# A Mamba-2 layer's gated norm: the last group's scale applied behind the output product, its squares added on GpSimd, and the mixer norm's two scales computed ahead of its tiles

## The chip, the cores and the metric

One core of a Trainium2 chip. Its engines are TensorE (PE, matrix products into PSUM), VectorE (DVE), ScalarE (ACT), GpSimd (POOL) and the engine that issues transfers (SP). Each runs its own row of instructions in a fixed order and waits on semaphores for the others. The metric is the device time of one execution in microseconds (us), the median of several runs.

## The reference

A two-layer decoder trunk on 576 tokens (512 of a prompt, 8 x 8 of samples), width 1024, float32. Layer 0 has a convolution and attention mixer, layer 1 a Mamba-2 mixer; behind each stands a convolutional feed-forward block. Cut to what the change touches:

```python
def rmsnorm(x, g):
    xf = x.astype(jnp.float32)
    xf = xf * lax.rsqrt(jnp.mean(xf * xf, axis=-1, keepdims=True) + EPS)
    return xf.astype(x.dtype) * g
...
def odd_mixer(h, conv_hist, ssm_hist, w_in, conv_w, conv_b, dt_bias, a_log, d_skip, gn_g, w_out):
...
    y, new_ssm = ssd_scan(xs, dt, a, bm, cm, ssm_hist)
    y = (y + d_skip[:, None] * xs).reshape(b, t, D_INNER) * jax.nn.silu(z)
    gs = D_INNER // SSM_GROUPS
    y = rmsnorm(y.reshape(b, t, SSM_GROUPS, gs), gn_g.reshape(SSM_GROUPS, gs)).reshape(b, t, D_INNER)
    return y @ w_out, new_conv, new_ssm
...
            dp, c1, s1 = odd_mixer(rmsnorm(xp, norm_mix_o[i]),
                                   jnp.zeros((bp, SSM_CONV_WIDTH - 1, SSM_CONV_DIM), dty),
                                   jnp.zeros((bp, SSM_HEADS, SSM_HEAD_DIM, SSM_STATE), dty), *ow)
...
        xp = xp + dp
...
        fp, f1 = conv_ffn(rmsnorm(xp, norm_ffn[layer]), jnp.zeros((bp, FFN_CONV_WIDTH - 1, D_FF), dty), *fw)
...
        xp = xp + fp
```

The gated norm is taken over each of 4 groups of 512 channels: its scale is one number per token and group. So is a norm's scale in general one number per token (`rs` below, 1/sqrt of the mean square); the gain (`g`, `gn`) is one per channel.

## The kernel before

**Layout.** Channels lie on the 128 partitions, tokens along the free dimension. The stream x is eight tiles `x0` to `x7` of 128 x 576, in SBUF throughout (`x_77` to `x_84` in the rows below). Work runs in two halves of 288 tokens (`HALF`).

**Products.** Each float32 operand is split into a rounded high part and the low rest: weights in `weights` (`wr` as loaded, `wh` by ACT at L163, `wl` by DVE at L164), activations by `split` (high by ACT at L193, low by DVE at L194). A product is three matmuls per 128 x 128 block (`mm3`, L173 high by high, L174 low of the activation, L175 low of the weight), each over 288 tokens into a PSUM tile called `mm`.

**A norm.** Squares are made by ACT (L225 for the first tile, L228 for others) and added up by DVE (L229, in `sq_add`). `rstd` then sums over partitions on PE (L202, with a column of ones), takes root and reciprocal in small pieces (ACT L209, DVE L210, ACT L211, DVE L212 to L214), spreads the result over the partitions on PE (L218) and copies it out (ACT L220): this is `rs`, or `grs` in the gate. In an *early* norm (that of the first mixer, and those of the feed-forward blocks, `norm_f1` among them) `norm_tile` splits x times the gain into `hh` and `hl` at once (ACT L248, DVE L249), and the scale is applied behind the product. In the mixer's norm `norm_o`, not early, `norm_half` waits for the scale, makes scaled tiles `hf` (DVE L261) and splits them (`hh` L193, `hl` L194). Before, it does so for half 0 as soon as that half's scale is there, then for half 1. `hf` itself goes into a plain float32 product for the time steps (`quarters`, L182).

**The mixer.** `mix1` goes over 4 groups. For each it runs the scan (`ssd`) on four tiles `xs`, beside it the matmuls of projections, then `gate`: y = `xs` times silu of z (DVE L1266), squares and `rstd`, y times gain times scale (DVE L1270), split into `yh` and `yl`. The output product of a group runs beside the next group's scan; that of the last group has nothing beside it but the second half of group 2's (four of its eight tiles).

**The last projection.** `out_proj` with `norm=True` takes the last group's y, four blocks deep: 12 matmuls for each of 16 half tiles. `add_x` adds the product out of PSUM to x (DVE L288), and `norm_tile` at once works on the new x for `norm_f1`: split and square. Tiles 0 to 3 go half by half, tiles 4 to 7 first in half 0, then in half 1, so that the first half's scale is ready early. Then `norm_half`, and the first gate products of the feed-forward block.

**What sets the order.** The instructions are written in one order, and a scheduler moves them within each engine's row; the order written is their priority. SBUF tiles of 576 tokens come from numbered slots by `S()` and go back by `free()`, the one idle longest first, so a new tile may wait for the last reader of the old one. PSUM tiles `mm` rotate through four banks in the last projection. The norms' small matmuls L202 and L218 stand in PE's row between the matmuls of products, which wait behind them if they wait.

Of the kernel before, what the change touches and what calls it, by code (L numbers as in the profile page):

```python
# [8 lines left out]
F32 = mybir.dt.float32  # L9
F32R = mybir.dt.float32r  # L10
AF = mybir.ActivationFunctionType
# [39 lines left out]
class Builder:  # L51
# [170 lines left out]
    def sq_add(self, acc, src, first, sl):  # L222
        nc = self.nc
        if first:
            nc.scalar.activation(acc[:, sl], src, AF.Square)  # L225
        else:
            t = self.S("sq")
            nc.scalar.activation(t[:, sl], src, AF.Square)  # L228
            nc.vector.tensor_tensor(acc[:, sl], acc[:, sl], t[:, sl], op=ADD)  # L229
            self.free(t)  # L230
# [10 lines left out]
    def norm_tile(self, m, sl):  # L241

        nc = self.nc
        x = self.x[m][:, sl]
        if self.early:
            g = self.pv(self.gname, m)
            h, l = self.h[m]
            nc.scalar.activation(h[:, sl], x, AF.Copy, scale=g)  # L248
            nc.vector.scalar_tensor_tensor(l[:, sl], x, g, h[:, sl].bitcast(F32), op0=MUL, op1=SUB)  # L249
        self.sq_add(self.ssq, x, m == 0, sl)  # L250

    def norm_half(self, half):
# [3 lines left out]
        if not self.early:  # L256
            for k in range(8):
                if half == 0:
                    self.hf.append(self.S("hf"))
                t = self.hf[k]  # L260
                nc.vector.scalar_tensor_tensor(t[:, sl], self.x[k][:, sl], self.pv(self.gname, k), self.rs[:, sl],  # L261
                                               op0=MUL, op1=MUL)
                self.split(t[:, sl], self.h[k], sl)
        if half == 1:
            self.free(self.ssq)

# [18 lines left out]
    def add_x(self, m, half, p):  # L285
        nc = self.nc
        sl = HALF[half]
        nc.vector.tensor_tensor(self.x[m][:, sl], self.x[m][:, sl], p[:, :HB], op=ADD)  # L288

    def out_proj(self, srcs, xs, kper, norm=False, last_y=False):  # L290
# [6 lines left out]
        for m, hf in order:  # L297
# [5 lines left out]
            self.add_x(m, hf, p)  # L303
# [550 lines left out]
    def mix1(self):  # L854
# [400 lines left out]
        def gate(g, yv):  # L1255
# [7 lines left out]
            for half in (0, 1):  # L1263
                sl = HALF[half]
                for t in range(4):
                    nc.vector.tensor_tensor(yv[t][:, sl], yv[t][:, sl], zs[t][:, sl], op=MUL)  # L1266
                    self.sq_add(ssq, yv[t][:, sl], t == 0, sl)
                self.rstd(rs, ssq, self.o512[:, 0:32], sl)
                for t in range(4):
                    nc.vector.scalar_tensor_tensor(yv[t][:, sl], yv[t][:, sl], self.pv("gn", 4 * g + t), rs[:, sl], op0=MUL, op1=MUL)  # L1270
                    self.split(yv[t][:, sl], ys[t], sl)
            self.free(ssq, rs, yv, zs)
# [56 lines left out]
        self.out_proj([d["w_out_o"][3, c] for c in range(4)], ys, 4, True)  # L1329
        self.free(ys)  # L1330
# [176 lines left out]
```

## Time and profile before

| what | value |
|---|---|
| runs | 1550.84, 1553.37, 1554.91 us; median 1553.37 |
| the profiled execution | 1553.1 us |
| its span, first to last instruction | 1551.3 us |
| mean granted clock of TensorE | 0.997 |
| norm ahead of the mixer | about 632 to 659 us of the span |
| the four scans and gates | 659 to 1101 us |
| last projection, with norm_f1's tiles | about 1101 to 1127 us |
| second feed-forward block | from 1127 us on |

The profile is of one execution, so sums are made against 1553.1. "Busy" is the share of time in which an engine has an instruction under way. In a row of the timeline stand the start, the length, the engine, the line, the operation with out and in, the shape, how many instructions in a row are folded together, and in brackets how long the engine had been idle before and whose result ended that. Matmuls overlap by about half, so the length of one (0.29 us) isn't what it costs.

Over the whole span PE's waits are short and few; the largest kinds are

```profile
PE yp L1148 <- DVE acb L1118: 7.2, 5, 2.4
PE mm L173 <- ACT wh L163: 5.5, 2, 5.4
PE pst L1200 <- ACT ysb L1191: 1.9, 2, 1.3
PE mm L175 <- DVE wl L164: 1.8, 2, 1.3
PE pr L218 <- DVE dg L214: 1.6, 3, 1.2
PE mm L173 <- DVE x L288: 1.4, 2, 1.1
```

(who waited, for whom, us in total, times, the longest). The first are in the scan, the second is the start of the program.

### The profile page before, as it was taken

The numbers are of one execution on the slowest core, as the hardware profiler recorded it, in microseconds if no ns is written. First come the engines' busy times: TensorE is split into PE (matmuls) and PEld (weight loads), VectorE is DVE, ScalarE is ACT, GpSimd is POOL, SyncE is SP. The second block draws the span as 40 slices with busy tenths as digits, with TensorE's granted clock in tenths as the row PEclk, the third lists the DMA queues.
The fourth block names the chain that finished last, engine by engine and source line by source line (L and its number), as shares of the span: only waits on it lengthen the run. The fifth ranks groups of instructions, "written<-read, shape, count | busy, mean of one in ns | idle before, by whom it ended". The sixth has DMA issues, their size and how long they took to land.

```text
span 1551.3 us, 28549 instructions
## 1 busy us (share of the span) xinstructions
PE 1520.5 (98%) x11635; PEld 1449.8 (93%) x11635; DVE 1018.5 (66%) x1805; ACT 649.3 (42%) x1232; POOL 154.7 (10%) x365
## 2 busy tenths in 40 slices
PE   8999999999999999999999999999999999999999
PEld 7977799999999999898988988998999999999999
DVE  7969887553555464678896786777976644663552
ACT  6356553221222222486855654646632222321220
POOL 0036001000000000011211112102010000000000
PEclk9999999999999999999999999999999999999999
DMA  8515223222222222136245245245222222223222
GB/s 239 136 42 131 85 70 98 86 86 85 83 77 78 92 82 85 55 104 202 71 148 180 83 115 185 72 125 173 87 84 85 91 83 82 82 73 92 82 87 75
DMA packets 69938, 157.80 MB, mean 102 GB/s; under 512 B 19871, under 2 KB 24607, under 8 KB 69807
## 3 DMA queue, kind: packets, MB, share of 16 engines
q1 hardware_dynamic: 69806, 155.97, 33.2%
q8 instruction: 92, 1.51, 0.4%
q14 instruction: 40, 0.32, 0.1%
HBM read 140.73 MB, written 15.21 MB: 101 GB/s over the span
## 4 chain that ended last, share of the span: by engine, by line
PE 88%; DVE 5%; ACT 4%; DMA 2%; issue 1%; SPq 0%; ACTq 0%; DVEq 0%
PE mm L173 27%; PE mm L175 27%; PE mm L174 26%; DMA acb<-acd 2%; PE yp L1148 1%; DVE wl L164 1%; ACT acb L1116 1%; PE mm L594 1%; ACT wh L163 1%; PE pst L1081 1%; PE pt L1063 1%; ACT sm L661 1%; PE py L1133 1%; PE pst L1200 1%; DMA out_ssm_s<-h 1%
## 5 line engine op out<-in xcount | busy, mean ns | idle before, releaser
L173 PE MATMUL mm<-hh,wh 128*128 128x288 f32 x2272 | 677.8, 299 | 6.8 <-ACT wh L163 5.5
L174 PE MATMUL mm<-hl,wh 128*128 128x288 f32 x2272 | 673.9, 297 | 0.7 <-DVE hl L389 0.4
L175 PE MATMUL mm<-hh,wl 128*128 128x288 f32 x2272 | 673.3, 297 | 0.5 <-DVE wl L164 0.4
L163 ACT ACTIVATE wh<-wr 128x1024 fp32r<-128x1024 f32 (+2 forms) x215 | 223.3, 1039 | 544.6 <-PE mm L174 275.1
L173 PEld LDWEIGHTS mm<-hh,wh 128*128 128x128 f32 x2272 | 428.3, 189 | 16.0 <-ACT wh L163 6.0
L174 PEld LDWEIGHTS mm<-hl,wh 128*128 128x128 f32 x2272 | 429.0, 189 | 4.8 <-issue 1.8
L175 PEld LDWEIGHTS mm<-hh,wl 128*128 128x128 f32 x2272 | 428.7, 189 | 3.2 <-issue 1.4
L164 DVE TENSOR_TENSOR wl<-wr,wh 128x1024 fp32r<-128x1024 f32 (+2 forms) x215 | 258.6, 1204 | 73.0 <-ACT wh L163 71.4
L173 PE MATMUL mm<-yh,wh 128*128 128x288 f32 x960 | 285.9, 298 | 1.5 <-DVE x L288 1.4
L175 PE MATMUL mm<-yh,wl 128*128 128x288 f32 x960 | 284.2, 297 | 1.3 <-DVE wl L164 1.3
L174 PE MATMUL mm<-yl,wh 128*128 128x288 f32 x960 | 285.3, 297 | 0.0
L173 PEld LDWEIGHTS mm<-yh,wh 128*128 128x128 f32 x960 | 181.1, 189 | 5.7 <-DVE x L288 2.5
L175 PEld LDWEIGHTS mm<-yh,wl 128*128 128x128 f32 x960 | 181.1, 189 | 2.4 <-DVE wl L164 1.6
L174 PEld LDWEIGHTS mm<-yl,wh 128*128 128x128 f32 x960 | 181.2, 189 | 1.5 <-issue 1.0
L288 DVE TENSOR_TENSOR x<-x,mm 128x288 f32<-128x288 f32 x192 | 84.9, 449 | 143.0 <-PE mm L175 142.8
L333 DVE TENSOR_TENSOR gbuf<-mm,rs 128x224 f32<-128x224 f32 x44 | 17.2, 391 | 108.6 <-PE mm L175 108.6
L344 ACT ACTIVATE gsilu<-gconv,par 128x512 f32<-128x512 f32 x44 | 31.8, 724 | 115.1 <-DVE gconv L341 115.1
L341 DVE SCALAR_TENSOR_TENSOR gconv<-gbuf,par,gconv 128x592 f32<-128x592 f32 x88 | 73.1, 831 | 1.5
L354 DVE TENSOR_TENSOR gsilu<-mm,gsilu 128x288 f32<-128x288 f32 x88 | 40.0, 454 | 50.5 <-PE mm L175 50.5
L880 DVE SCALAR_TENSOR_TENSOR cconv<-cbuf,par,cconv 128x600 f32<-128x600 f32 x72 | 59.6, 838 | 10.1 <-ACT cconv L878 9.5
L336 POOL COPY fpo<-gbuf 128x2 f32<-128x2 f32 x44 | 12.4, 281 | 476.0 <-DVE gbuf L333 476.0
L1116 ACT ACTIVATE acb<-acb,ac 128x128 f32<-128x128 f32 x128 | 41.4, 390 | 35.6 <-DMA acb<-acd 25.0
(322 smaller groups left out, 1593.6 us busy)
## 6 DMA issues: line engine op xcount, KB each, us to landing
wr<-in_w_gate SPq DMA_DIRECT2D x44, 512.0 KB, 3.5
wr<-in_w_up SPq DMA_DIRECT2D x44, 512.0 KB, 3.5
wr<-in_w_in_o SPq DMA_DIRECT2D x40, 512.0 KB, 3.6
wr<-in_w_down SPq DMA_DIRECT2D x32, 448.0 KB, 3.3
wr<-in_w_down SPq DMA_DIRECT2D x16, 512.0 KB, 3.5
h<-in_h SPq DMA_DIRECT2D x32, 256.0 KB, 3.1
acb<-acd SPq DMA_DIRECT2D x32, 256.0 KB, 4.2
out_ssm_s<-h SPq DMA_DIRECT2D x32, 256.0 KB, 2.6
```

The costliest lines, as they stand in the source:

```text
L163: nc.scalar.activation(hi[:, a:b], raw[:, a:b], AF.Copy)
L164: nc.vector.tensor_tensor(lo[:, a:b], raw[:, a:b], hi[:, a:b].bitcast(F32), op=SUB)
L173: nc.tensor.matmul(out, hi[:, ws], xh[:, sl], start=i == 0, stop=False)
L174: nc.tensor.matmul(out, hi[:, ws], xl[:, sl], start=False, stop=False)
L175: nc.tensor.matmul(out, lo[:, ws], xh[:, sl], start=False, stop=i == n - 1)
L288: nc.vector.tensor_tensor(self.x[m][:, sl], self.x[m][:, sl], p[:, :HB], op=ADD)
L333: nc.vector.tensor_tensor(g[:, 290:514], p[:, 0:224], rs[:, HB:NP], op=MUL)
L341: nc.vector.scalar_tensor_tensor(cv[:, :592], g[:, k:592 + k], w(k), cv[:, :592], op0=MUL, op1=ADD)
L344: nc.scalar.activation(sl[:, :NP], cv[:, :NP], AF.Silu, bias=b)
L354: nc.vector.tensor_tensor(sl[:, HALF[half]], p[:, :HB], sl[:, HALF[half]], op=MUL)
L880: nc.vector.scalar_tensor_tensor(cv[:, :600], g[:, k:600 + k], w(k), cv[:, :600], op0=MUL, op1=ADD)
L1116: nc.scalar.activation(acb[:, cs], acb[:, cs], AF.Relu, bias=ac[:, o:o + 1], scale=-1.0)
```

## The change

Four edits:

- In the gate of the last group (`g == 3`) y is no longer multiplied by its scale. y times the gain is split at once (ACT L1275, DVE L1276 in the new numbering), and the scale `grs` is kept as `self.yrs` and given to `out_proj`. There `add_x` multiplies the product by it as it leaves PSUM (DVE L290, into a tile `xt`) and adds that to x in a second instruction (DVE L291). The other groups keep the old way.
- The squares of that gate are added on GpSimd instead of DVE (6 adds of 128 x 288).
- Those of `norm_f1` too (14 adds of 128 x 288).
- In `norm_half` of the mixer norm the tiles of both halves are written behind the scale of half 1; so both scales rank ahead of the tiles.

DVE goes from 1807 to 1795 instructions, GpSimd from 370 to 390; ACT, PE and SP keep their numbers.

```diff
@@ -219,14 +219,14 @@
         self.free(rv, dg)
         nc.scalar.activation(out[:, sl], pr[:, :HB], AF.Copy)
 
-    def sq_add(self, acc, src, first, sl):
+    def sq_add(self, acc, src, first, sl, eng=None):
         nc = self.nc
         if first:
             nc.scalar.activation(acc[:, sl], src, AF.Square)
         else:
             t = self.S("sq")
             nc.scalar.activation(t[:, sl], src, AF.Square)
-            nc.vector.tensor_tensor(acc[:, sl], acc[:, sl], t[:, sl], op=ADD)
+            (eng or nc.vector).tensor_tensor(acc[:, sl], acc[:, sl], t[:, sl], op=ADD)
             self.free(t)
 
 
@@ -247,22 +247,22 @@
             h, l = self.h[m]
             nc.scalar.activation(h[:, sl], x, AF.Copy, scale=g)
             nc.vector.scalar_tensor_tensor(l[:, sl], x, g, h[:, sl].bitcast(F32), op0=MUL, op1=SUB)
-        self.sq_add(self.ssq, x, m == 0, sl)
+        self.sq_add(self.ssq, x, m == 0, sl, nc.gpsimd if self.gname == "norm_f1" else None)
 
     def norm_half(self, half):
         nc = self.nc
         sl = HALF[half]
         self.rstd(self.rs, self.ssq, self.o1024, sl)
-        if not self.early:
-            for k in range(8):
-                if half == 0:
-                    self.hf.append(self.S("hf"))
-                t = self.hf[k]
-                nc.vector.scalar_tensor_tensor(t[:, sl], self.x[k][:, sl], self.pv(self.gname, k), self.rs[:, sl],
-                                               op0=MUL, op1=MUL)
-                self.split(t[:, sl], self.h[k], sl)
         if half == 1:
             self.free(self.ssq)
+            if not self.early:
+                self.hf = [self.S("hf") for _ in range(8)]
+                for sl in HALF:
+                    for k in range(8):
+                        t = self.hf[k]
+                        nc.vector.scalar_tensor_tensor(t[:, sl], self.x[k][:, sl], self.pv(self.gname, k), self.rs[:, sl],
+                                                       op0=MUL, op1=MUL)
+                        self.split(t[:, sl], self.h[k], sl)
 
     def norm_end(self):
         self.free(self.rs, self.h)
@@ -282,12 +282,18 @@
                         self.quarters(p, w, HALF[half])
                     evac(half, p)
 
-    def add_x(self, m, half, p):
+    def add_x(self, m, half, p, scale=None):
         nc = self.nc
         sl = HALF[half]
+        if scale is not None:
+            t = self.S("xt", HB)
+            nc.vector.tensor_tensor(t, p[:, :HB], scale[:, sl], op=MUL)
+            nc.vector.tensor_tensor(self.x[m][:, sl], self.x[m][:, sl], t, op=ADD)
+            self.free(t)
+            return
         nc.vector.tensor_tensor(self.x[m][:, sl], self.x[m][:, sl], p[:, :HB], op=ADD)
 
-    def out_proj(self, srcs, xs, kper, norm=False, last_y=False):
+    def out_proj(self, srcs, xs, kper, norm=False, last_y=False, scale=None):
 
         mper = 8 // len(srcs)
         ws = {}
@@ -300,7 +306,7 @@
                 ws[c] = self.weights(srcs[c], mper * kper * P)
             p = self.pm()
             self.mm3(p[:, :HB], ws[c], [(m % mper) * kper + k for k in range(kper)], xs, HALF[hf])
-            self.add_x(m, hf, p)
+            self.add_x(m, hf, p, scale)
             if norm:
                 self.norm_tile(m, HALF[hf])
                 if m == 7:
@@ -1264,12 +1270,22 @@
                 sl = HALF[half]
                 for t in range(4):
                     nc.vector.tensor_tensor(yv[t][:, sl], yv[t][:, sl], zs[t][:, sl], op=MUL)
-                    self.sq_add(ssq, yv[t][:, sl], t == 0, sl)
+                    if g == 3:
+                        gn, (yh, yl) = self.pv("gn", 4 * g + t), ys[t]
+                        nc.scalar.activation(yh[:, sl], yv[t][:, sl], AF.Copy, scale=gn)
+                        nc.vector.scalar_tensor_tensor(yl[:, sl], yv[t][:, sl], gn, yh[:, sl].bitcast(F32), op0=MUL, op1=SUB)
+                    self.sq_add(ssq, yv[t][:, sl], t == 0, sl, nc.gpsimd if g == 3 else None)
                 self.rstd(rs, ssq, self.o512[:, 0:32], sl)
+                if g == 3:
+                    continue
                 for t in range(4):
                     nc.vector.scalar_tensor_tensor(yv[t][:, sl], yv[t][:, sl], self.pv("gn", 4 * g + t), rs[:, sl], op0=MUL, op1=MUL)
                     self.split(yv[t][:, sl], ys[t], sl)
-            self.free(ssq, rs, yv, zs)
+            self.free(ssq, yv, zs)
+            if g == 3:
+                self.yrs = rs
+            else:
+                self.free(rs)
             return ys
 
         def run(main, side):
@@ -1326,8 +1342,8 @@
         self.norm_end()
         self.norm_begin("norm_f1", True)
         self.rings = {"mm": [0, 1, 2, 3], "aux": [4, 5, 6, 7]}
-        self.out_proj([d["w_out_o"][3, c] for c in range(4)], ys, 4, True)
-        self.free(ys)
+        self.out_proj([d["w_out_o"][3, c] for c in range(4)], ys, 4, True, scale=self.yrs)
+        self.free(ys, self.yrs)
```

**DVE at the mixer norm.** DVE's row before, from the low parts of half 0's middle tiles on; `x_77` to `x_84` are the eight tiles of x, `rv` and `dg` belong to the rstd, `wl` to weights:

```order
L194 TENSOR_TENSOR hl<-hf,hh 128x288 x4
L261 SCALAR_TENSOR_TENSOR hf<-x_82,par,rs 128x288
L261 SCALAR_TENSOR_TENSOR hf<-x_83,par,rs 128x288
L261 SCALAR_TENSOR_TENSOR hf<-x_84,par,rs 128x288
L194 TENSOR_TENSOR hl<-hf,hh 128x288 x3
L229 TENSOR_TENSOR ssq<-ssq,sq 128x288
L288 TENSOR_TENSOR x_84<-x_84,mm 128x288
L164 TENSOR_TENSOR wl<-wr,wh 128x1024
L229 TENSOR_TENSOR ssq<-ssq,sq 128x288
L921 MEMSET sp_v 128x32
L210 RECIPROCAL rv<-rv 128x72
L212 TENSOR_SCALAR rv<-rv,rsc 128x72
```

and now, from the first low part of half 0 on:

```order
L194 TENSOR_TENSOR hl<-hf,hh 128x288
L263 SCALAR_TENSOR_TENSOR hf<-x_79,par,rs 128x288
L263 SCALAR_TENSOR_TENSOR hf<-x_80,par,rs 128x288
L229 TENSOR_TENSOR ssq<-ssq,sq 128x288
L194 TENSOR_TENSOR hl<-hf,hh 128x288 x2
L210 RECIPROCAL rv<-rv 128x72
L194 TENSOR_TENSOR hl<-hf,hh 128x288
L212 TENSOR_SCALAR rv<-rv,rsc 128x72
L263 SCALAR_TENSOR_TENSOR hf<-x_81,par,rs 128x288
L213 SCALAR_TENSOR_TENSOR rv<-dg,rsc,rv 128x72
L263 SCALAR_TENSOR_TENSOR hf<-x_82,par,rs 128x288
L214 TENSOR_TENSOR dg<-rv,rsc 128x288
```

The last add of squares (L229) and the rstd's four operations (L210 to L214) of half 1 stood behind all of half 0's tiles and an L164; now they stand among half 0's first tiles, and the L164 behind all sixteen.

**DVE in the last projection**, tiles 3 to 5. Before:

```order
L229 TENSOR_TENSOR ssq<-ssq,sq 128x288
L288 TENSOR_TENSOR x_80<-x_80,mm 128x288 x2
L164 TENSOR_TENSOR wl<-wr,wh 128x1024
L249 SCALAR_TENSOR_TENSOR hl<-x_80,par,hh 128x288
L229 TENSOR_TENSOR ssq<-ssq,sq 128x288
L249 SCALAR_TENSOR_TENSOR hl<-x_80,par,hh 128x288
L229 TENSOR_TENSOR ssq<-ssq,sq 128x288
L288 TENSOR_TENSOR x_81<-x_81,mm 128x288
L288 TENSOR_TENSOR x_82<-x_82,mm 128x288
L164 TENSOR_TENSOR wl<-wr,wh 128x1024
```

now (L294 and L288 are the same line of `add_x`, of which L290 and L291 are the new branch):

```order
L290 TENSOR_TENSOR xt<-mm,grs 128x288 x2
L291 TENSOR_TENSOR x_79<-x_79,xt 128x288 x2
L290 TENSOR_TENSOR xt<-mm,grs 128x288
L249 SCALAR_TENSOR_TENSOR hl<-x_79,par,hh 128x288
L291 TENSOR_TENSOR x_80<-x_80,xt 128x288
L249 SCALAR_TENSOR_TENSOR hl<-x_79,par,hh 128x288
L290 TENSOR_TENSOR xt<-mm,grs 128x288
L249 SCALAR_TENSOR_TENSOR hl<-x_80,par,hh 128x288
L291 TENSOR_TENSOR x_80<-x_80,xt 128x288
L164 TENSOR_TENSOR wl<-wr,wh 128x1024
L249 SCALAR_TENSOR_TENSOR hl<-x_80,par,hh 128x288
```

Each L288 became an L290 and an L291, and each L229 left DVE's row.

**GpSimd from the last scan into the last gate and projection** (`h` are states of the scan, `gbuf` a buffer of the next block, `fhist` its history). Before:

```order
L1176 TENSOR_TENSOR h_12081<-h_12081,cds 128x512
L1176 TENSOR_TENSOR h_12083<-h_12083,cds 128x512
L1176 TENSOR_TENSOR h_12079<-h_12079,cds 128x512
L327 MEMSET gbuf 128x2 x2
L328 COPY gbuf<-fhist 128x8x2 x3
```

now:

```order
L1182 TENSOR_TENSOR h_12083<-h_12083,cds 128x512
L1182 TENSOR_TENSOR h_12079<-h_12079,cds 128x512
L229 TENSOR_TENSOR gssq<-gssq,sq 128x288 x6
L229 TENSOR_TENSOR ssq<-ssq,sq 128x288
L333 MEMSET gbuf 128x2
L334 COPY gbuf<-fhist 128x8x2
L229 TENSOR_TENSOR ssq<-ssq,sq 128x288
L333 MEMSET gbuf 128x2
```

The gate's six adds and the projection's fourteen now stand ahead of or among the small preparations (a memset and a copy each) of the next block. Towards the end of the projection three such pairs stand in a row ahead of the last three adds, those of tiles 5 to 7 in half 1; two of the three write into slots that held `yh` and `yl`.

## The prediction

> **What bounds the kernel now.** The page first: one core, and the share of each engine.
>
> ```profile
> span 1551.3 us, 28549 instructions
> PE 1520.5 (98%) x11635; PEld 1449.8 (93%) x11635; DVE 1018.5 (66%) x1805; ACT 649.3 (42%) x1232; POOL 154.7 (10%) x365
> ```
>
> TensorE is busy 1520.5 of 1551.3 us, and the change leaves its number of matmuls as it was. So the whole prize is PE's lost time, at most 30.8 us over the program. (A busy PE may still be waiting inside a row, as shown below.) DVE's 66% is a mean over stages; the windows of the stages that are edited say more (columns: window, its length, then the busy time of PE, of PE's weight loads, of DVE, ACT and POOL, the granted clock and the DMA share):
>
> ```profile
> 637.00:659.00 22.00, 19.79 (x145) 16.19 (x143) 17.45 (x42) 10.32 (x26) 1.01 (x4) 0.92 0.19 65
> 1075.00:1101.00 26.00, 23.19 (x182) 21.22 (x182) 24.34 (x59) 12.06 (x25) 1.64 (x7) 0.93 0.21 73
> 1101.00:1128.00 27.00, 27.00 (x210) 26.70 (x210) 26.10 (x60) 18.89 (x41) 2.01 (x9) 1.00 0.31 98
> ```
>
> The first is the norm ahead of the Mamba mixer: PE idles 2.2 us. The second is the last gate: PE idles 2.8 us. The third is the last output projection with the squares of the last norm: PE never idles, but DVE is busy 26.10 of 27.00 us. There is nothing to win for PE there, and next to nothing left on DVE.
>
> **The mixer norm.** PE and then DVE in the first window (start, length, idle time before it and what ended it):
>
> ```profile
> 638.42 0.53 PE L173 MATMUL mm<-hh,wh 128*128 128x288 f32 x2 [0.32 <-ACT hh L193]
> 642.65 1.18 PE L182 MATMUL mm<-hf,wr 128*32 128x288 f32 x16
> 646.59 0.33 PE L202 MATMUL pt<-ssq,o 128*32 128x72 f32 x8
> 647.62 0.53 PE L917 MATMUL pt<-cst,dtr 128*128 128x32 f32 x4
> 649.31 0.40 PE L218 MATMUL pr<-dg,l 128*128 128x288 f32 x1 [1.17 <-DVE dg L214]
> 656.45 0.69 PE L182 MATMUL mm<-hf,wr 128*32 128x288 f32 x8
> 658.32 0.69 PE L182 MATMUL mm<-hf,wr 128*32 128x288 f32 x8
> ```
>
> ```profile
> 637.38 1.37 DVE L261 SCALAR_TENSOR_TENSOR hf<-x,par,rs 128x288 f32<-128x288 f32 x3
> 642.72 1.19 DVE L194 TENSOR_TENSOR hl<-hf,hh 128x288 fp32r<-128x288 f32 x3
> 645.70 0.45 DVE L229 TENSOR_TENSOR ssq<-ssq,sq 128x288 f32<-128x288 f32 x1
> 647.34 0.60 DVE L210 RECIPROCAL rv<-rv 128x72 f32<-128x72 f32 x1 [1.16 <-ACT rv L209]
> 650.19 1.38 DVE L261 SCALAR_TENSOR_TENSOR hf<-x,par,rs 128x288 f32<-128x288 f32 x3 [0.94 <-ACT rs L220]
> 658.20 0.46 DVE L194 TENSOR_TENSOR hl<-hf,hh 128x288 fp32r<-128x288 f32 x1 [0.51 <-ACT hh L193]
> ```
>
> The squares of half 1 are added late, at 645.70, since they stand behind all of half 0's tiles. From there to 650.19 DVE only waits along the chain L202, L209, L210, L214, L218, L220. How fast can PE go? These two rows stand 22 matmuls apart:
>
> ```profile
> 1128.12 0.30 PE L174 MATMUL mm<-hl,wh 128*128 128x288 f32 x1
> 1131.03 0.29 PE L175 MATMUL mm<-hh,wl 128*128 128x288 f32 x1
> ```
>
> That is 2.91 / 22 = 0.132 us each. From 638.42 to 659.01 PE issues 90 such matmuls (11.9 us) and the L182, L202, L917 and L218 rows above (2.56 + 0.33 + 0.53 + 0.40), 15.7 us of 20.6. So 4.9 us are lost, more than the 2.2 us that show as idle.
>
> After the change the add and the rstd of half 1 run among half 0's tiles, and the dead 4.5 us go. DVE's new row, from 637.38 on: 16 hf at 0.43 (three in 1.37 us, less the last one's pipelined end), 16 hl at 0.37, two adds and an x at 0.37, the rstd's four (0.52 + 0.20 + 0.25 + 0.37), 15.3 us; the last hl ends near 652.7 instead of 658.66. PE needs the last hf for L182, and I put the end of the second L182 group at 653.3. By then 73 matmuls are out instead of 90, and L917 isn't; these cost 17 x 0.132 + 0.36 = 2.6 us more. So 659.0 - 653.3 - 2.6 = 3.1 us; I take **-3.0**. Bounds: 0.5 gained (the weight rows that now stand behind the norm come late, or the reordered first SSD group waits) to 4.9 (every loss goes).
>
> **The last gate.** PE's waits there, all of them:
>
> ```profile
> 1084.17 0.41 PE L173 MATMUL mm<-yh,wh 128*128 128x288 f32 x1 [0.34 <-DVE x L288]
> 1088.95 0.40 PE L173 MATMUL mm<-yh,wh 128*128 128x288 f32 x1 [1.08 <-DVE x L288]
> 1093.75 0.40 PE L175 MATMUL mm<-yh,wl 128*128 128x288 f32 x1 [1.35 <-DVE wl L164]
> ```
>
> 2.77 us: DVE is full, so evictions (L288) and weight parts (L164) come late. The change takes 6 adds (0.37 us each at DVE's pace) off DVE, and the split of y no longer waits for the rstd, since the scale is applied in the projection. But L202, which sums the squares, stands in PE's row with matmuls behind it, and now waits for GpSimd's three adds of a half: at 0.73 us each (worked out below) against 0.37 that is 1.1 us later, 1.3 with the first add's start behind its square; at the second half 0.8, since PE is busier ahead of it. The eviction L294 behind the rstd's small operations costs about 0.7 as before, a weight part about 0.3. That is 3.1 us of waits that come for 2.77 that go: **+0.3**, between -2.8 (no wait comes) and +0.9.
>
> **The last output projection.** Prices from groups of the page (mean ns before the last bar):
>
> ```profile
> L288 DVE TENSOR_TENSOR x<-x,mm 128x288 f32<-128x288 f32 x192 | 84.9, 449 | 143.0 <-PE mm L175 142.8
> L229 DVE TENSOR_TENSOR ssq<-ssq,sq 128x288 f32<-128x288 f32 x42 | 18.9, 451 | 3.6 <-ACT sq L228 3.6
> L249 DVE SCALAR_TENSOR_TENSOR hl<-x,par,hh 128x288 fp32r<-128x288 f32 x32 | 16.1, 508 | 0.6 <-ACT hh L248 0.5
> L164 DVE TENSOR_TENSOR wl<-wr,wh 128x1024 fp32r<-128x1024 f32 x181 | 222.3, 1229 | 61.0 <-ACT wh L163 59.5 <-PE pyo L1170 1.5
> L1176 POOL TENSOR_TENSOR h<-h,cds 128x512 f32<-128x512 f32 x32 | 40.4, 1292 | 133.9 <-PE pyo L1170 133.9
> L1153 DVE TENSOR_TENSOR xs<-xs,ea 128x384 f32<-128x384 f32 x16 | 10.8, 673 | 0.0
> L1266 DVE TENSOR_TENSOR xs<-xs,zs 128x288 f32<-128x288 f32 x32 | 15.3, 506 | 2.2 <-ACT zs L1262 2.2
> ```
>
> A half tile is 12 matmuls, 1.59 us of PE; 16 of them, 25.4 us. On DVE it now costs L290 (out of PSUM like L288, 0.37 at pace), L291 (needs L290, so its full 0.45) and L249 (0.43): 1.25 us instead of 1.23 with the add (L288, L249, L229). Sixteen of these and 4 or 5 L164 make 25 to 26 us, level with PE. The 14 adds that left paid for the 16 instructions that came, no more. So a microsecond that DVE loses is soon one that PE loses, as four PSUM banks go round.
>
> What may make DVE lose it is GpSimd. No row shows a 128x288 add there; by elements it is 1292 x 288/512 = 0.73 us (estimate). Its company shows in another stage, four GpSimd adds beside DVE's work, twice, and a small copy beside one L164:
>
> ```profile
> 928.04 4.81 POOL L1176 TENSOR_TENSOR h<-h,cds 128x512 f32<-128x512 f32 x4 [26.51 <-PE pyo L1170]
> 930.84 1.12 DVE L1153 TENSOR_TENSOR xs<-xs,ea 128x384 f32<-128x384 f32 x1
> 931.88 0.44 DVE L288 TENSOR_TENSOR x<-x,mm 128x288 f32<-128x288 f32 x1
> 932.24 1.70 DVE L164 TENSOR_TENSOR wl<-wr,wh 128x1024 fp32r<-128x1024 f32 x1
> 955.53 5.70 POOL L1176 TENSOR_TENSOR h<-h,cds 128x512 f32<-128x512 f32 x4 [13.80 <-PE pyo L1170]
> 959.03 1.29 DVE L1266 TENSOR_TENSOR xs<-xs,zs 128x288 f32<-128x288 f32 x1
> 1099.95 1.22 DVE L164 TENSOR_TENSOR wl<-wr,wh 128x1024 fp32r<-128x1024 f32 x1
> 1100.05 1.18 POOL L328 COPY gbuf<-fhist 128x16 f32<-128x16 f32 x1
> ```
>
> A 128x288 multiply of two SBUF tiles (L1266) took 1.29 us where its mean is 0.51, L1153 1.12 instead of 0.67, an L164 1.70 instead of 1.23; L288, which reads PSUM, kept its 0.44. The copy lasted as long as the L164. [...] An add delays DVE by 0 (it runs beside L290, or DVE was waiting anyway) to 0.73 us. I take 0.3, the 0.73 less the 0.37 of an L290 that can run beside it: 14 x 0.3 = 4.2. The longer chain to the norm's L202 (L290, L291, square, add instead of L288, square, add), and GpSimd's gbuf rows, which now stand among its adds (two of them wait for the last y matmuls, with three adds queued behind), cost perhaps 1.1 with DVE free, mostly within the same stalls; DVE's half-1 gate rows, done earlier, give some back. **+4.0**, between 0 and 10.2.
>
> [...]
>
> **Sum.** 1553.1 (the profiled execution, 1551.3 of span and 1.8 around it) - 3.0 + 0.3 + 4.0 = 1554.4. The median of the three runs lies 0.3 higher, at 1553.37, so I say 1554.5.
>
> **Rivals.**
> *GpSimd's adds are hidden.* They fall beside L290, or grow longer themselves and leave DVE alone, as the copy of 1.18 us did. For it: L288 kept its 0.44, and PE has four banks ahead. Against it: DVE has under 1 us to spare. 1553.1 - 3.0 + 0.3 + 0 = 1550.4, with all of the norm's 4.9 us 1548.5.
> *Every add blocks DVE for its full length*, slower than before: 14 x 0.73 = 10.2 us at the projection, 1553.1 - 3.0 + 0.3 + 10.2 = 1560.6. For it: 1.29 against 0.51, a loss of 0.78. Against it: in the 4.81 us from 928.04 DVE lost only 0.45 + 0.47 = 0.92, so each of the four adds, 1.2 us long, cost 0.23; a shorter one should not cost more, though DVE's work there was less dense. It decides from a mean delay of about 0.5 us per add: 14 x 0.5 - 2.7 = 4.3.
> *The norm's reorder gains nothing*, since what follows (weights, the scan's first chain) takes it back: 1553.1 + 0.3 + 4.0 = 1557.4. For it, the weights come no sooner, and DVE already waits for them behind this stretch:
>
> ```profile
> 661.00 1.22 DVE L164 TENSOR_TENSOR wl<-wr,wh 128x1024 fp32r<-128x1024 f32 x1 [2.34 <-ACT wh L163]
> ```
>
> Against it: PE's losses stand within the stretch itself, and 4.5 us of them are DVE waiting for one chain.
>
> **How the numbers follow.** A measurement of this kernel tells about 0.3%, 4.7 us, from no change: faster is below 1548.7, slower above 1558.0. The forecast, with 2 to 6 us for GpSimd, has 0.50 and lies within. Hidden adds 0.25, of it 0.06 below 1548.7. Full blocking 0.13, all above 1558.0. No gain at the norm 0.12, of it 0.03 above. So faster 0.06, same 0.78, slower 0.16. The range leaves out the lowest of the second case and the upper half of the third: 1549.0 to 1560.0.
>
> **What would show it.** The norm: the second L182 group about 5 us earlier against the last y matmul before it, and no hf group that waits for rs behind a dead DVE. The gate: PE idle 2 to 3.7 us between 1075 and 1101, at L202 and L294. The projection: GpSimd adds of 0.6 to 1.2 us, L291 and L249 above 0.45 and 0.51, and waits of PE for L290 where there was none; if these rows keep their lengths, the first rival holds. The prediction is wrong if the adds cost nothing and the scan's first group gains too, or if GpSimd, by waiting for DVE, holds the norm's L202 for several us.

## The result, and the profile after

| | median, us | lowest to highest | runs |
|---|---|---|---|
| before | 1552.11 | 1549.25 to 1554.91 | 4 |
| changed | 1560.39 | 1559.66 to 1560.95 | 4 |

The ratio is 1.0054, with a 95% interval of 1.0036 to 1.0071: the change costs about 8 us. The forecast was 1554.5, in a range of 1549 to 1560.

The page of the changed kernel has the same number of matmuls and almost the same busy time on PE and DVE; GpSimd has 20 us more:

```profile
span 1557.9 us, 28571 instructions
PE 1522.2 (98%) x11635; PEld 1452.0 (93%) x11635; DVE 1020.5 (66%) x1793; ACT 649.1 (42%) x1232; POOL 174.6 (11%) x385
```

What is new shows in the list of PE's waits (who waited for whom, us in total, times, longest). Neither of the first two lines exists before:

```profile
PE pt L202 <- POOL ssq L229: 5.2, 2, 3.9
PE pt L202 <- POOL gssq L229: 1.9, 1, 1.9
PE mm L173 <- DVE x L294: 1.8, 2, 1.5
```

PE waits 7.1 us at L202, the sums of squares, for GpSimd's adds. To compare stages between runs, whose starts differ by a us or two, PE's matmuls are counted in the timeline from the same point on: from the first L202 of the mixer norm to the first L202 of the first gate, and, in the last gate, from the first y matmul behind the last state update (L1200, now L1206). From there group 2 has 96 y matmuls left, the last projection 192, then the next block's h matmuls follow. Times in us behind that point; "idle" and "half clock" are PE's loss from there to the 100th h, the first from one-microsecond windows, the second, an estimate, as the sum of PE's busy time times one minus the granted clock in them:

| kernel | norm to first gate | 96th y | 192nd y | 288th y | 100th h | idle | half clock |
|---|---|---|---|---|---|---|---|
| before | 124.6 | 19.2 | 32.0 | 45.1 | 58.9 | 2.8 | 1.7 |
| changed | 121.5 | 20.8 | 33.5 | 52.2 | 67.6 | 9.7 | 3.4 |

So the norm gained 3.1 us and the last gate and projection lost 8.7. The rest, 1.0, is spread: +1.8 ahead of the norm, -1.5 in the scans, +0.7 behind. Together that is the 6.6 us between the spans.

**The norm.** PE's rows after:

```profile
640.62 0.54 PE L173 MATMUL mm<-hh,wh 128*128 128x288 f32 x2 [0.70 <-ACT hh L193]
642.70 0.33 PE L202 MATMUL pt<-ssq,o 128*32 128x72 f32 x8
646.01 0.40 PE L218 MATMUL pr<-dg,l 128*128 128x288 f32 x1
654.92 0.69 PE L182 MATMUL mm<-hf,wr 128*32 128x288 f32 x8
```

From the first h matmul to the last L182 it took 15.0 us, where it took 20.6, with 17 matmuls fewer in between. L218's wait of 1.17 us is gone. There is a second gain, which the busy share hides. One window of before and one of after (window, length, busy of PE, PE's loads, DVE, ACT and POOL, and third from the end the granted clock):

```profile
651.00:652.00 1.00, 1.00 (x7) 1.00 (x6) 1.00 (x4) 1.00 (x3) 0.00 (x0) 0.50 0.00 0
...
651.00:652.00 1.00, 1.00 (x10) 1.00 (x9) 1.00 (x4) 0.38 (x2) 0.00 (x0) 1.00 0.00 0
```

Before, PE got half its clock for 3 us right behind its waits: 7 matmuls fall into a microsecond that looks fully busy, instead of 10 when all goes well, and they start 0.24 us apart (651.20, 651.44, 651.68) instead of 0.13. That cost 1.7 us; the idle time fell by 1.2 (2.2 to 1.0).

**Gate and projection.** PE's waits in the last gate, and at the two sums of `norm_f1`:

```profile
1086.69 0.33 PE L202 MATMUL pt<-gssq,o 128*32 128x72 f32 x8 [1.86 <-POOL gssq L229]
1088.53 0.40 PE L173 MATMUL mm<-yh,wh 128*128 128x288 f32 x1 [1.51 <-DVE x L294]
1094.13 0.40 PE L175 MATMUL mm<-yh,wl 128*128 128x288 f32 x1 [0.72 <-DVE wl L164]
...
1125.86 0.33 PE L202 MATMUL pt<-ssq,o 128*32 128x72 f32 x8 [3.93 <-POOL ssq L229]
1137.03 0.33 PE L202 MATMUL pt<-ssq,o 128*32 128x72 f32 x8 [1.29 <-POOL ssq L229]
```

and what GpSimd and DVE did just ahead of the 3.93 us:

```profile
1121.60 1.75 POOL L229 TENSOR_TENSOR ssq<-ssq,sq 128x288 f32<-128x288 f32 x2
1124.71 1.09 POOL L229 TENSOR_TENSOR ssq<-ssq,sq 128x288 f32<-128x288 f32 x1 [0.75 <-ACT sq L228]
...
1121.88 0.83 DVE L249 SCALAR_TENSOR_TENSOR hl<-x,par,hh 128x288 fp32r<-128x288 f32 x1
1122.63 1.04 DVE L291 TENSOR_TENSOR x<-x,xt 128x288 f32<-128x288 f32 x1
```

L249 and L291 take 0.83 and 1.04 us beside the two adds, 0.50 and 0.45 otherwise. The late L291 makes the last square late, the add behind it takes 1.09 us, and L202 waits for it with 27 y matmuls queued behind. Lateness is not all of it. Before, half 0's last add and its sum were

```profile
1123.57 0.45 DVE L229 TENSOR_TENSOR ssq<-ssq,sq 128x288 f32<-128x288 f32 x1
1124.16 0.33 PE L202 MATMUL pt<-ssq,o 128*32 128x72 f32 x8
```

Counted from the 96th y, that add ended at 22.8 us, and it ends at 25.7 now, 2.9 later. And the sum stood behind 269 of the 288 y matmuls and stands behind 261 now, since the scheduler set it sooner: 8 matmuls of 0.132 us, 1.1 us. Together they make about the wait. Then the clock falls again:

```profile
1127.00:1128.00 1.00, 1.00 (x7) 1.00 (x6) 1.00 (x3) 1.00 (x2) 0.94 (x3) 0.59 0.00 0
```

### The profile page after: what moved, and what is told of

Read it like the earlier page. It is cut to its first block, busy times and chain, and to the rows that moved or that the text cites. A ratio compares the mean times of both kernels' runs of the same rounds, so it can differ in the third digit from the quotient of the medians.

```text
span 1557.9 us, 28571 instructions
## 1 busy us (share of the span) xinstructions
PE 1522.2 (98%) x11635; PEld 1452.0 (93%) x11635; DVE 1020.5 (66%) x1793; ACT 649.1 (42%) x1232; POOL 174.6 (11%) x385
## 3 DMA queue, kind: packets, MB, share of 16 engines
q1 hardware_dynamic: 69806, 155.97, 32.6%
q8 instruction: 92, 1.51, 0.4%
## 4 chain that ended last, share of the span: by engine, by line
PE 86%; DVE 6%; ACT 4%; DMA 2%; issue 1%; POOL 0%; SPq 0%; ACTq 0%; DVEq 0%; POOLq 0%
PE mm L173 26%; PE mm L175 26%; PE mm L174 26%; DMA acb<-acd 1%; DVE wl L164 1%; PE yp L1154 1%; ACT wh L163 1%; ACT acb L1122 1%; PE mm L600 1%; PE pt L1069 1%; PE py L1139 1%; ACT sm L667 1%; PE pst L1087 1%; DVE ca L480 0%; PE po L710 0%
## 5 line engine op out<-in xcount | busy, mean ns | idle before, releaser
L164 DVE TENSOR_TENSOR wl<-wr,wh 128x1024 fp32r<-128x1024 f32 (+2 forms) x215 | 259.2, 1206 | 74.7 <-ACT wh L163 73.6
L294 DVE TENSOR_TENSOR x<-x,mm 128x288 f32<-128x288 f32 x176 | 78.0, 449 | 143.4 <-PE mm L175 143.3
L1182 POOL TENSOR_TENSOR h<-h,cds 128x512 f32<-128x512 f32 x32 | 41.6, 1330 | 140.5 <-PE pyo L1176 140.5
```

The costliest lines, as they stand in the source:

```text
L164: nc.vector.tensor_tensor(lo[:, a:b], raw[:, a:b], hi[:, a:b].bitcast(F32), op=SUB)
L1182: nc.gpsimd.tensor_tensor(hp(h0[bh][b4]), hp(h0[bh][b4]), cds[:, b * 32 + 8 * g:b * 32 + 8 * g + 8].unsqueeze(2).broadcast_to([P, 8, 64]), ...
```

## The experiments

Each was timed in five rounds beside the kernel before; ratios are to that. The kernel before had medians of 1552.22 us beside e1 to e4, 1551.30 beside e5 to e8, 1550.98 beside e9 to e11 and 1550.09 beside e12, so kernels of different batches are compared by ratio and not by median. Their stages, counted as above:

| kernel | ratio, 95% interval | 96th y | 192nd y | 288th y | 100th h | idle | half clock |
|---|---|---|---|---|---|---|---|
| e1 order alone | 0.9988, 0.9979 to 0.9997 | 19.2 | 31.9 | 45.1 | 58.9 | 2.8 | 1.7 |
| e2 scale alone | 1.0033, 1.0021 to 1.0045 | 22.7 | 35.4 | 48.6 | 62.7 | 4.8 | 3.1 |
| e3 GpSimd alone | 1.0073, 1.0061 to 1.0085 | 18.0 | 36.7 | 52.0 | 67.2 | 9.8 | 1.6 |
| e4 order, scale | 1.0027, 1.0015 to 1.0039 | 22.6 | 35.3 | 48.5 | 62.5 | 4.9 | 3.1 |
| e5 e4, gate's adds on GpSimd | 1.0020, 1.0008 to 1.0032 | 22.6 | 35.3 | 48.4 | 62.5 | 3.8 | 4.7 |
| e6 e4, idle adds | 1.0041, 1.0027 to 1.0054 | 23.7 | 36.5 | 54.2 | 70.2 | 9.3 | 5.9 |
| e7 e4, split behind | 1.0029, 1.0016 to 1.0043 | 23.6 | 36.3 | 49.4 | 63.4 | 6.5 | 3.0 |
| e8 changed, late sums | 1.0046, 1.0029 to 1.0063 | 20.8 | 33.5 | 46.2 | 66.5 | 9.0 | 3.3 |
| e9 e4, late rstd | 1.0001, 0.9991 to 1.0011 | 18.2 | 32.6 | 45.8 | 59.8 | 3.3 | 1.5 |
| e10 e9, gate's adds on GpSimd | 1.0005, 0.9992 to 1.0017 | 21.1 | 34.4 | 47.6 | 61.7 | 5.3 | 2.0 |
| e11 e1, gate's adds on GpSimd | 1.0034, 1.0021 to 1.0047 | 19.0 | 38.1 | 51.7 | 65.4 | 6.0 | 4.7 |
| e12 changed, sums apart | 1.0069, 1.0054 to 1.0083 | 22.6 | 35.3 | 48.0 | 69.5 | 8.0 | 7.4 |

Each row of stages is of one execution. Half clock comes and goes between executions: in the scans, which no experiment changes, it came to between 0 (e2, e6) and 4.9 us (e10). So a difference of 1 to 3 us in the last column, and what it adds to the times, may be chance.

The first four take the change apart.

**e1: the mixer norm's order alone.** The change's `norm_half` on the kernel before, nothing else:

```diff
     def norm_half(self, half):
...
+            if not self.early:
+                self.hf = [self.S("hf") for _ in range(8)]
+                for sl in HALF:
+                    for k in range(8):
```

> The kernel before with one edit alone: in the mixer norm both scales rank ahead of the tiles. In the changed kernel's trace PE stood 1.8 us later than before at the first L202 of this norm and 1.3 us earlier at the first L202 of the first gate, so this edit gained 3.1 us there. Both theories: 2.5 to 3.5 us below the kernel before. The rival that what follows takes it back: within 1 us of it.

Measured 1550.08 us, 0.12% below before, some 2 us (0.5 to 3.3): less than the 2.5 to 3.5 of both theories and more than the rival's 1. The stage took 121.5 us, as in the changed kernel. The edit gains and keeps it. How much depends on the clock: e2 and e3 have the old norm, lost 2.2 and 2.4 us of idle time there, and saw no half clock; their stage took 123.2 and 123.4 us. So the profiles put 1.2 to 1.9 us on the waits, and 1.7 more when the clock falls.

**e2: the scale's move alone; e3: the adds on GpSimd alone; e4: order and scale, adds on DVE.**

```diff
-        self.sq_add(self.ssq, x, m == 0, sl, nc.gpsimd if self.gname == "norm_f1" else None)
+        self.sq_add(self.ssq, x, m == 0, sl)
...
-                    self.sq_add(ssq, yv[t][:, sl], t == 0, sl, nc.gpsimd if g == 3 else None)
+                    self.sq_add(ssq, yv[t][:, sl], t == 0, sl)
```

(e4 against the changed kernel; e2 has the old `norm_half` besides; e3 is the kernel before with these lines the other way round.)

> The kernel before with the last group's scale applied behind the product (L290, L291), all squares added on DVE, the mixer norm as before. Theory 1 (the loss is GpSimd's adds holding DVE up, and the scale's move by itself costs little): within 2 us of the kernel before. Theory 2 (the loss is the scale's two instructions for one, on a full DVE, and the longer way to the sums at L202): 4 to 6 us above it, with PE waiting 3 us or more at L202 for DVE's add.

> The kernel before with the 20 adds on GpSimd alone; scale and mixer norm as before. Theory 1: 5 to 9 us above the kernel before, with two-input DVE rows beside the adds at 0.8 to 1.1 us instead of 0.45. Theory 2: DVE is relieved of 20 adds (9 us of its work), so at most 1 us above it, or below it.

> The changed kernel with all squares added on DVE again (the mixer norm's order and the scale's move stay). Theory 1: 1 to 3 us below the kernel before. Theory 2: 1 to 3 us above it. In both, DVE's rows beside no GpSimd add keep 0.45 us.

Measured 1556.72, 1563.17 and 1555.25 us. Both theories are half right. e2 lies in theory 2's band, though PE waits only 1.4 us at L202 in it; e3 lies above theory 1's band; e4 lies above before, as theory 2 had it. The scale's move alone costs 0.33%, the adds alone 0.73%, and the two together less than their sum: with the order, 0.54%. The table puts the scale's price where neither theory had it: 3.5 of e2's 3.8 us are there at the 96th y, in the gate. From the 96th to the 288th y e2 and e4 need 25.9 us, as before: in the projection two instructions for one cost nothing. They do make the sums late. In e4 half 0's last add ends 24.6 us behind the 96th y, 1.8 later than before:

```profile
1126.37 0.45 DVE L229 TENSOR_TENSOR ssq<-ssq,sq 128x288 f32<-128x288 f32 x1
1127.16 0.33 PE L202 MATMUL pt<-ssq,o 128*32 128x72 f32 x8
```

But the scheduler set this sum behind 285 y matmuls instead of 269, and half 1's behind 59 h matmuls instead of 30, and PE waits at neither. PE's rows of e4 in the gate:

```profile
1086.03 0.33 PE L202 MATMUL pt<-gssq,o 128*32 128x72 f32 x8 [0.86 <-DVE gssq L229]
1087.87 0.40 PE L173 MATMUL mm<-yh,wh 128*128 128x288 f32 x1 [1.51 <-DVE x L294]
1092.22 0.33 PE L202 MATMUL pt<-gssq,o 128*32 128x72 f32 x8 [0.89 <-DVE gssq L229]
1094.71 0.40 PE L175 MATMUL mm<-yh,wl 128*128 128x288 f32 x1 [1.23 <-DVE wl L164]
```

PE is held at both sums, which it was not before; DVE's splits of y now stand among the products and adds that the sums wait for (e7 moves them). Idle time rose by 2.1 us, half clock by 1.4.

**e5: norm_f1's adds back on DVE, the gate's on GpSimd.** The first pair of lines of the diff above.

> The changed kernel with norm_f1's 14 adds on DVE again; the gate's 6 adds stay on GpSimd. If the loss beside the scale's move is the 14 adds in the projection: PE needs about 26 us from the 96th to the 288th y matmul, as with all adds on DVE, and the time is 1551 to 1553 us. If the gate's adds are to blame too: 1556 us or more.

Measured 1554.82 us, 0.20% above before. The projection is that of e4. So of the changed kernel's 8.7 us the 14 adds of `norm_f1` cost 5.1 (67.6 less 62.5). The gate didn't get the 20.8 us that it had in the changed kernel: the profiled execution had the half clock there for 10 us, with less idle time than e4. In the profile that makes 1.8 us, about what the time misses 1551 to 1553 by; whether the other executions had it too isn't shown.

**e6: GpSimd's company without its results.** e4, with an extra add beside each of the 14.

```diff
             nc.vector.tensor_tensor(acc[:, sl], acc[:, sl], t[:, sl], op=ADD)
+            if idle is not None:
+                nc.gpsimd.tensor_tensor(idle[:, sl], t[:, sl], t[:, sl], op=ADD)
```

> The kernel with the new order and the scale's move and all real adds on DVE (1555.25 us), and beside each of norm_f1's 14 adds an extra 128x288 add on GpSimd, of the same squares, into a tile that nobody reads. PE's sums (L202) wait for DVE alone, so only GpSimd's company is left. If GpSimd holds DVE up: L291, L249 and L229 rows beside it at 0.8 to 1.1 us, and 3 us or more above 1555.25. If the loss is that L202 waits for GpSimd's own, later result: within 1 us of 1555.25.

Measured 1558.78 us. DVE's groups in the projection, three of e4 and two of e6 (mean ns before the last bar):

```profile
L249 DVE SCALAR_TENSOR_TENSOR hl<-x,par,hh 128x288 fp32r<-128x288 f32 x16 | 8.2, 514 | 0.2
L291 DVE TENSOR_TENSOR x<-x,xt 128x288 f32<-128x288 f32 x16 | 6.9, 450 | 0.0
L229 DVE TENSOR_TENSOR ssq<-ssq,sq 128x288 f32<-128x288 f32 x14 | 6.3, 453 | 0.0
...
L299 DVE TENSOR_TENSOR x<-x,xt 128x288 f32<-128x288 f32 x16 | 8.8, 562 | 0.0
L230 DVE TENSOR_TENSOR ssq<-ssq,sq 128x288 f32<-128x288 f32 x14 | 8.6, 617 | 0.0
```

Adds that nobody waits for lengthen L291 from 0.45 to 0.56 us on average and the real adds from 0.45 to 0.62, and PE is 7.7 us later at the 100th h. GpSimd's company alone holds DVE up. The timed loss is smaller, 0.14% of the ratios or some 2 us, short of the 3 that were forecast: of the 7.7 us 2.8 are half clock, and this execution had none of it in the scans, where e4's had 1.7. In the changed kernel the same groups are:

```profile
L249 DVE SCALAR_TENSOR_TENSOR hl<-x,par,hh 128x288 fp32r<-128x288 f32 x16 | 10.5, 655 | 0.4 <-ACT hh L248 0.2
L291 DVE TENSOR_TENSOR x<-x,xt 128x288 f32<-128x288 f32 x16 | 8.8, 562 | 0.0
L290 DVE TENSOR_TENSOR xt<-mm,grs 128x288 f32<-128x288 f32 x16 | 7.0, 449 | 3.4 <-PE mm L175 3.0 <-issue 0.3
L164 DVE TENSOR_TENSOR wl<-wr,wh 128x1024 fp32r<-128x1024 f32 x5 | 6.7, 1338 | 0.6 <-ACT wh L163 0.6
L229 POOL TENSOR_TENSOR ssq<-ssq,sq 128x288 f32<-128x288 f32 x14 | 13.1, 938 | 23.9 <-ACT sq L228 23.8
```

DVE lost 2.3 us at L249, 1.9 at L291 and 0.6 at L164 (e4's five took 6.1), 4.8 us for 14 adds, and got rid of 6.3 us of adds. L290, which reads PSUM, kept its 0.45. So DVE was not busier than in e4. What got worse is the time until a result is there: an add takes 0.94 us instead of 0.45, and the L291 ahead of it may be the one that stood still.

**e7: the gate's split written behind its squares.** e4, with yh and yl of a half behind its `rstd`:

```diff
-                    if g == 3:
-                        gn, (yh, yl) = self.pv("gn", 4 * g + t), ys[t]
...
                 self.rstd(rs, ssq, self.o512[:, 0:32], sl)
                 if g == 3:
+                    for t in range(4):
+                        gn, (yh, yl) = self.pv("gn", 4 * g + t), ys[t]
...
                     continue
```

> The kernel with the new order and the scale's move and all adds on DVE (1555.25 us), with the last gate's split of y written behind its squares and rstd instead of ahead of each square. There the gate took 3.5 us more than before, with DVE's splits (L1276) between the adds that L202 waits for. If this place is the cost of the scale's move: the 96th y matmul is out 2 to 4 us sooner, 1551 to 1553 us. If it is the two instructions for one as such: 1554 to 1556 us.

Measured 1556.36 us. The scheduler answered by setting both halves' sums behind the same 36 y matmuls, and PE waited longer there:

```profile
1090.94 0.47 PE L202 MATMUL pt<-gssq,o 128*32 128x72 f32 x8 [3.96 <-DVE gssq L229]
```

The splits' place does make the adds late: counted from the first y, the last add of half 0 ended at 5.5 us instead of e4's 6.3, and that of half 1 at 9.8 instead of 12.5. But half 1's sum, which stood behind 50 y matmuls in e4, now stood behind 36, and that undid it. So two things count: when the adds are done, and what PE has behind a sum that isn't ready.

**e8: the sums of norm_f1 behind the last y matmul**, in the changed kernel.

```diff
-                if m == 7:
-                    self.norm_half(hf)
+                if m == 7 and (hf == 1 or self.gname != "norm_f1"):
+                    for half in ((0, 1) if self.gname == "norm_f1" else (hf,)):
+                        self.norm_half(half)
```

> The changed kernel, but PE's sums of norm_f1 (L202 of both halves) are written behind the last y matmul instead of half 0's ahead of the last 27. If most of the loss in the projection is PE held at L202 by GpSimd's late add (3.9 us in the profile): 3 us or more below 1560.39, with the 288 y matmuls out about 4 us sooner. If it is DVE's lost time: within 1.5 us of 1560.39, the wait turning up at evictions or later sums.

Measured 1559.92 us, as changed. The 288 y matmuls were out 6.0 us sooner, so DVE keeps up with PE in the projection even beside GpSimd (25.4 us from the 96th to the 288th y); but at the 100th h 1.1 us were left of it:

```profile
1127.39 0.33 PE L202 MATMUL pt<-ssq,o 128*32 128x72 f32 x8 [0.40 <-POOL ssq L229]
1135.10 0.42 PE L202 MATMUL pt<-ssq,o 128*32 128x72 f32 x8 [4.00 <-POOL ssq L229]
```

The wait of 4 us went from the first half's sum to the second's. There GpSimd's result is no later than DVE's was in e4 (half 1's last add ends 33.4 us behind the 96th y, in e4 33.7), but the sum stands behind 24 h matmuls where e4 had 59 ahead of it.

**e9 and e10: the last gate's rstd behind group 2's products.** e4, where the moved scale isn't needed before the first L290; e10 has the gate's adds on GpSimd besides.

```diff
                 for f in ot[4:]:
                     f()
+                for sl in HALF:
+                    self.rstd(self.yrs, self.yssq, self.o512[:, 0:32], sl)
```

> The kernel with the new order and the scale's move and all adds on DVE (3.0 us above before), with the rstd of the last gate (L202, L210 to L218) written behind the last products of group 2, where the moved scale allows it. If the 3.6 us that the scale's move cost in the gate are PE held at L202 behind a longer DVE chain, and the half clock that follows such idle time: the 96th y matmul is out 2 to 3.5 us sooner and the time is within 1 us of the kernel with the new order alone (about 2 us below before). If DVE is simply short of time there: the wait moves to evictions or to L290, and the time stays 2 us or more above before.

> As the last one, with the gate's 6 adds on GpSimd. If DVE is short of time in the gate: 1 to 2 us below the last one. If GpSimd's adds cost DVE as much as they save (rows of 0.8 to 1.1 us instead of 0.45): within 1 us of it.

Measured 1550.23 and 1552.85 us, ratios 1.0001 and 1.0005. PE's waits of e9:

```profile
1085.28 0.33 PE L202 MATMUL pt<-gssq,o 128*32 128x72 f32 x8 [0.86 <-DVE gssq L229]
1087.12 0.61 PE L173 MATMUL mm<-yh,wh 128*128 128x288 f32 x1 [1.50 <-DVE x L294]
1099.34 0.40 PE L173 MATMUL mm<-yh,wh 128*128 128x288 f32 x1 [0.50 <-ACT grs L220]
```

The second half's sum no longer holds PE, and the weight part comes in time: 2.7 of the scale's 3.6 us come back, half of them as clock. From the 96th to the 192nd y it needs 14.4 us instead of 12.7, a wait of 0.50 us for `grs` among them. By the ratios e9 is 0.13%, or 2 us, above e1 and level with before, between the two forecasts. So most of the price of the scale's move was where its sums stood. e10 is 0.04% above e9 by the ratios and 2.6 us by the medians, and in its profile PE waits 3.0 us at an eviction; either way the gate's adds gain nothing on GpSimd when nothing hangs on them.

**e11: the gate's adds on GpSimd with the scale left in the gate.** On e1, with `sq_add` taking an engine as in the change:

```diff
-                    self.sq_add(ssq, yv[t][:, sl], t == 0, sl)
+                    self.sq_add(ssq, yv[t][:, sl], t == 0, sl, nc.gpsimd if g == 3 else None)
```

> The new order of the mixer norm and the gate's 6 adds on GpSimd, nothing else changed (scale in the gate, norm_f1's adds on DVE). If the adds' later result and GpSimd's company cost in the gate too: 2 us or more above the kernel with the new order alone, which is about 2 us below before. If they relieve DVE: at or below it.

Measured 1555.74 us, 0.34% above before, some 7 us above e1. PE's two longest waits there:

```profile
1087.00 0.33 PE L202 MATMUL pt<-gssq,o 128*32 128x72 f32 x8 [2.69 <-POOL gbuf L327]
1099.92 0.40 PE L173 MATMUL mm<-yh,wh 128*128 128x288 f32 x1 [1.40 <-ACT yh L193]
```

(L327 is the row next to the third add, which ended at 1086.94.) The first three adds took 3.99 us, and the sum waited for them. From the 96th to the 192nd y it takes 19.2 us instead of 12.7: y waits for its scale, with 2.7 us of waits, and PE then runs at half clock for 7 us, which costs some 3. With the scale moved the same six adds cost nothing (e5 against e4). That fits e3's place as the slowest of the first four: the scale's move, a loss alone, takes away most of what these adds cost.

**e12: the sums of norm_f1 about as late as with the adds on DVE.** The changed kernel with half 0's `norm_half` behind the last tile and half 1's behind the next block's products of half 0 (`todo_half` is set in `out_proj`, behind half 0's):

```diff
             for half in (0, 1):
+                if half == 1 and self.todo_half:
+                    self.norm_half(1)
+                    self.todo_half = False
                 for w, (src, m, evac) in zip(ws, grp):
```

> The changed kernel (all 20 adds on GpSimd, scale moved, new order) with PE's sums of norm_f1 set about as late as they stand with the adds on DVE: half 0's behind the last y matmul, half 1's behind 72 matmuls of the next block. If the 5.1 us that norm_f1's adds on GpSimd cost are PE held at sums that stand too early for GpSimd's late result: no wait at L202 there, and 3 to 6 us below the changed kernel (1554 to 1557 us). If GpSimd takes so much of DVE's time that PE waits in any order: within 2 us of the changed kernel.

Measured 1561.56 us. L202 hardly waits, but the next matmul of the same chain does:

```profile
1129.20 0.33 PE L203 MATMUL pt<-ssq,o 128*32 128x72 f32 x8 [0.18 <-POOL ssq L230]
1138.69 0.61 PE L219 MATMUL pr<-dg,l 128*128 128x288 f32 x1 [4.05 <-DVE dg L215]
```

(L203 and L219 are L202 and L218.) Between them lie ACT's and DVE's small operations, queued behind tiles that are themselves late, and a weight part of 1.81 us beside two adds: 9.5 us from the sum to L219, where e4 needs 3.5. The adds themselves are done about when e4's are (25.5 and 33.2 us behind the 96th y, in e4 24.6 and 33.7). An order of the sums that avoids the wait was not found; whether there is one stays open.

## Why the prediction was wrong

- **The norm, -3.0.** Right in size, 3.1 in the profile and about 2 in the timed runs. But its 4.9 us of loss were read as waiting inside busy rows; 1.7 of them were half clock, which is not always there.
- **The gate, +0.3.** Mis-sized: 1.6 us at the 96th y in the changed kernel's profile, above its bound of +0.9, and 3.4 there for the scale's move with the adds on DVE. L202 was put at 1.3 and 0.8 us and took 1.86 and none. The evictions were put at 0.7 "as before", though the prediction's own row shows 1.08, and took 1.85 in two; the weight part was put at 0.3 and took 0.72. So the step that failed is the claim that the split of y "no longer waits for the rstd" and so relieves DVE. It does come sooner, but ahead of adds and evictions that PE waits for: with the splits behind (e7) the adds were done 0.9 and 2.8 us sooner. With the rstd further back (e9) 2.7 us return.
- **The projection, +4.0.** Mis-sized too: 5.4 us between the 96th and the 288th y, and 1.6 to the 100th h. (The parts named there, 4.2 and 1.1, come to 5.3; no row gave the size of what was taken off for their overlap.) The price of an add on DVE was right, 0.3 forecast and 4.8 / 14 = 0.34 measured. Its source was the author's estimate only: no run shows an add that delays DVE by 0.73 us less the 0.37 of an L290; the adds themselves took 0.79 to 1.15 us, 0.94 on average. But it was added to PE's time as if DVE were the bound there. DVE got as much back as it lost, and e8's y matmuls ran at full pace. The failing step is the term priced at "perhaps 1.1", the longer chain to L202: PE stood there 5.2 us. Half 0's last add came 2.9 us later than before, 1.8 of it with the adds on DVE (e4) and 1.1 by GpSimd, and the forecast took the sum's place in PE's row as given, while the scheduler moved it. How the loss divides between late results and the sums' places stays open: e8 and e12 set the sums later, and the wait turned up further on.
- **A term was missing**: the half clock behind waits, 3.4 us in this stage against 1.7 before. It came behind the 3.93 us at L202 (granted clock 0.50 from 1128 to 1130 us) and not behind the 1.29 us there.
- **The second rival** gave 1560.6, close to the result, but by another way: not 0.73 us of DVE's time per add. That the time fits does not make the mechanism right. The first rival is wrong as well, since the adds are not hidden; e1 speaks against the third, with a gain of 0.5 to 3.3 us.
- **GpSimd's gbuf rows** were part of that same "1.1". At the second sum they made most of the wait of 1.29 us: the last square was ready at 1135.06, its add began at 1135.91, behind a copy that ran beside an L164 (ACT, GpSimd twice, DVE):

```profile
1134.63 0.43 ACT L228 ACTIVATE sq<-x 128x288 f32<-128x288 f32 x1
1134.80 1.16 POOL L334 COPY gbuf<-fhist 128x16 f32<-128x16 f32 x1
1135.91 1.06 POOL L229 TENSOR_TENSOR ssq<-ssq,sq 128x288 f32<-128x288 f32 x1
1134.07 1.83 DVE L164 TENSOR_TENSOR wl<-wr,wh 128x1024 fp32r<-128x1024 f32 x1
```

The best of these kernels is e1, the order alone: 0.12% below before (interval 0.03% to 0.21%), and below the changed kernel by 0.66% of their ratios.

## What to carry to other kernels

Moving an add off a full engine shortens that engine's list (here by 6.3 us of adds in the projection, of which 4.8 came back at its other instructions), but a sum that the matmul engine waits for in its own row sees only when the result is there (0.94 us for an add instead of 0.45, and PE 7.1 us at L202); price the last link of the chain, and what is queued behind it. Work that is made ready sooner than needed can push back what is needed now (the splits of y, 0.9 and 2.8 us at the adds of e4 against e7). And an idle gap on the matmul engine may cost nearly as much again in clock (1.7 us beside 2.2 of idle time in the norm before, none beside 2.2 and 2.4 in e2 and e3), so read the granted clock in windows as short as the gap.

## What the runs showed of the hardware

- **The clock.** PE ran at a granted clock of 0.50 for some us behind waits. In the kernel before from 651 to 654 us, behind waits of 1.17 and 0.50 us, and from 1095 to 1098, behind one of 1.35; in the changed kernel from 1090 to 1093, behind 1.86 and 1.51, and from 1128 to 1130, behind 3.93; in e9 from 1087 to 1090, behind 0.86 and 1.50; in e5's gate for 10 us. Matmuls start 0.24 us apart then instead of 0.13. Behind the 1.29 us at the changed kernel's second sum the clock stayed at 1.00. The same norm with about the same idle time had it once (2.2 us, before) and twice not (2.2 and 2.4 us, e2 and e3). What starts and ends it no run shows.
- **GpSimd beside DVE.** In the changed kernel's projection a 128x288 add on GpSimd took 0.79 us at its shortest, 0.94 on average and 1.15 at its longest. L291 and L249, DVE's operations with two SBUF inputs, took up to 1.07 and 1.11 us there, where e4 has 0.45 and 0.51 on average; L290, which reads PSUM, kept 0.45 on average, as in e4, e5, e6 and e8. It can also be the add that takes longer: at 1120.12 us one took 1.15, while the L291 beside it kept 0.45, and in e11's gate one took 2.26 us, while DVE's L1266 beside it, also with two SBUF inputs, kept 0.45.
